# Layer B's transposition transfers issued by two queues, and its products with probabilities one sub-block later

## The chip, the cores and the metric

The kernel runs on one core of a Trainium2 chip. The core has five engines with instruction streams of their own: TensorE (PE in the profile, its weight loads PEld), VectorE (DVE), ScalarE (ACT), GpSimd (POOL) and SyncE (SP). Transfers run on 16 DMA engines; an engine's stream issues them, and the profile shows such issues with a q behind the engine's name (SPq, ACTq), those of GpSimd as POOL. The metric is the device time of one execution in microseconds (us), as the median of several runs.

## The reference

Two transformer layers over 256 positions of width 2048, with 32 heads of 128. Layer A has chunked attention with a relative bias. Layer B, the one that is changed, has "forgetting attention" against keys and values that come from a projection of their own:

```python
h_kv = rms_norm(x, kv_norm)
k_s, v_s = jnp.split(h_kv @ kv_w, 2, axis=-1)
logf = jax.nn.log_sigmoid((h_kv @ f_w + f_b).astype(jnp.float32))
cum_logf_h = jnp.transpose(jnp.cumsum(logf, axis=1), (0, 2, 1))
...
q, g = jnp.split(h @ b_w_in[lb], 2, axis=-1)
sc = einsum('bqhd,bkhd->bhqk', q_b, k_b) * scale + decay     # causal, decay from cum_logf_h
o = einsum('bhqk,bkhd->bqhd', softmax(sc), v_b)              # blocks of 128 queries
x = x + (o * silu(g)) @ b_w_out[lb]
```

All is in float32. The large products are made of three matmuls each, since every operand is split into a high part that TensorE takes whole and a low remainder: high by high, high by low, low by high.

## The kernel before

The kernel streams the weights once. Each layer's input projection is cut into 16 groups of two heads. A group has two **units** of 512 columns: in layer A `aqk` (queries and keys) and `avg` (values and gate), in layer B `bqg` (queries and gate) and `bkv` (keys and values). A unit has eight **sub-blocks** of 256 rows of the inner dimension, of 512 KB of weights each. From the second group on, seven of them are plain, and the eighth sub-blocks of the two units are done together as a **quad** (class `Quad`, lines 279 to 352): sums and differences of weight halves are formed, and fewer matmuls do both.

The way of a sub-block: SyncE issues its load (line 208) into one of six buffers `raw`; ScalarE makes the high part `hi` (line 244 in layer B, with the norm's gain; line 249 in A), VectorE the low part `lo` (line 245 or 250), each in one of four buffers, and TensorE multiplies (line 186). Splits are kept three sub-blocks ahead of TensorE. For the quad, ScalarE scales the raw weights (line 297), VectorE forms differences (lines 299, 300, 308, 309), and four splits follow (`quad_hi` line 305, `quad_lo` line 306).

Attention of a group runs as a side job, a Python generator that is advanced between the sub-blocks of later units. `side_b` (line 918) and `attention` (line 547) have these steps, each up to a `yield`:

1. `evac_scaled` copies the keys out, scaled (line 523), `turn` (line 509) transposes queries and keys: VectorE transposes 32 x 32 blocks into `first` (line 514), then sixteen transfers move the blocks into place in `sums` (line 517). The biases (lines 927, 928, 930) belong to this step.
2. `v_split` (lines 626 to 628): the values, split, into `vh`, `vl` and `v1`.
3. `split_pairs` (lines 535, 536): queries and keys split into `wide` and `q1`, and `q0` (line 559).
4. The scores: matmuls into `s1p` (lines 543 to 545) and `s0p` (line 567), then the first half of the softmax (lines 577 to 584), and its second half in a step of its own.
5. The gate is scaled by the softmax's sums (line 594), and a second `turn` transposes probabilities and gate together (from `sgY` to `sgZ`, again sixteen transfers).
6. `split` of the probabilities into `wide` (lines 535, 536).
7. The products with the probabilities into `op` (lines 543 to 545, 607).
8. The gate's multiplication and the split of the result (lines 611, 616, 617).

Where they run is set by hand. `drive` (line 744) advances a side by so many steps behind a sub-block. In layer B, `B1_STEPS = {3: 1, 5: 1, 6: 2}` puts step 2 behind sub-block 3 of the next group's first unit, step 3 behind sub-block 5, step 4 behind sub-block 6; `B2_STEPS = {1: 1}` puts step 5 into that group's second unit; `OLD_B_STEPS = {0: 1, 1: 99}` puts step 6 behind sub-block 0 of the first unit of the group after that, and steps 7 and 8 behind sub-block 1. The last two groups' sides run within the output projection (`project`, line 1022), with lists of counts.

The program's order in the code is not fully the order on the engines: an instruction may be moved ahead in its engine's stream where its data seem ready. Two devices bind it. `feed.behind` (line 264) writes a two-element copy of a weight split into a tile, so that what fills this tile comes behind that split; its place counts among the splits that are ready (0 to 2). `tc.issue_after(x)` puts what is traced within it behind `x` on the same engine, without an instruction. `feed.by_act` is ScalarE's last traced weight split.

Queues: in layer A, the first transposition's transfers go out by four queue entries (GpSimd three, ScalarE one), one for each `j`; in layer B all sixteen of both transpositions are issued by GpSimd. At a group's end, `add_whole` (line 731) adds the quad's part, held in `comb`, to the whole unit's result (VectorE, 128 x 512, line 735, twice), and `evac_scaled` then scales the keys (ScalarE, 128 x 256, line 523, twice).

Of the kernel before, what the change touches and what calls it, by code (L numbers as in the profile page):

```python
# [13 lines left out]
OP = mybir.AluOpType  # L14
# [4 lines left out]
NT = S // P  # L19
# [41 lines left out]
OLD_A_STEPS = {1: 1, 3: 99}  # L61
B1_STEPS = {3: 1, 5: 1, 6: 2}
B2_STEPS = {1: 1}
OLD_B_STEPS = {0: 1, 1: 99}
FORGET_STEPS = {0: 1, 2: 1, 6: 1, 7: 1}


def r32(ap):
    return ap.bitcast(F32)
# [8 lines left out]
def trunk(ctx, tc, x, x_t, gains, a_w_in, a_rel, a_w_out, kv_w, f_w, f_b, b_w_in, b_w_out, final_norm, out):  # L78
# [111 lines left out]
    class Feed:  # L190
# [73 lines left out]
        def behind(self, dst, n):  # L264

            act.activation(dst, r32(self.ready[n][0][:, 0, :, :1]), AF.Copy)

        def fill(self):
            while len(self.ready) <= DEPTH:
# [200 lines left out]
    def rest(u):  # L470

        for b in range(u.done, u.plain):
            u.step(b)
            yield u.acc
# [50 lines left out]
    def split_pairs(many, place=None):  # L525

        out = []
        for srcs, tag in many:
            out.append(att.tile([P, srcs[0].shape[1], 2, len(srcs), P], F32R, name=tag, tag=tag))
            if place is not None:  # L530
                feed.behind(out[-1][:, 0, 0, :, :1], place)
        for k in range(len(many[0][0])):
            for (srcs, _), both in zip(many, out):
                h, l = (both[:, :, i, k].rearrange("p t (i u) -> p t i u", u=SQ) for i in range(2))
                act.activation(h, srcs[k], AF.Copy)
                dve.tensor_sub(l, srcs[k], r32(h))  # L536
        return [[both[:, :, i].rearrange("p t k n -> p k n t") for i in range(2)] for both in out]

# [5 lines left out]
        pe.matmul(out_, a[0], b[1], start=False, stop=False)  # L544
        pe.matmul(out_, a[1], b[0], start=False, stop=stop)  # L545

    def attention(g, biases, qk, vg, half, ocat, queues=(pool,) * NQ, line=(None, None), home=None):


        z = turn(qk.rearrange("p t (c d) -> p (t c) d", d=DH), NT * 2 * HG, "qk", queues, home)  # L550
        bias1, bias0 = biases()
        qkT = z.rearrange("p i (t c) u -> p c t i u", t=NT)
        yield
        (kh, kl), (qh, ql) = split_pairs([([qkT[:, HG + i] for i in range(HG)], "wide"),
                                          ([qkT[:, i, 1:] for i in range(HG)], "q1")], line[0])
        q0 = att.tile([P, HG, P], F32, name="q0", tag="oT")
        if line[0] is not None:
            feed.behind(q0[:, :, :1], line[0])
        act.activation(q0.rearrange("p h (i u) -> p h i u", u=SQ),
                       qkT[:, :HG, 0], AF.Copy)  # L560
        yield
        s1p = bank("s1p")[:, :].rearrange("p (i s) -> p i s", i=HG)
        s0p = bank("s0p")[:, :HG * P].rearrange("p (i s) -> p i s", i=HG)
        for i in range(HG):
            dot3(s1p[:, i], (qh[:, i, :, 0], ql[:, i, :, 0]), (kh[:, i], kl[:, i]))
        for i in range(HG):
            pe.matmul(s0p[:, i], q0[:, i], qkT[:, HG + i, 0], start=True, stop=True)
        NB = 1 + NT
        sg = att.tile([P, HG * NB + NT * HG, P], F32, name="sg", tag="R")
        sv = sg[:, :HG * NB].rearrange("p (i c) k -> p i (c k)", i=HG)  # L570
        nm = small.tile([P, NT, HG], F32, name="nm")
        sm = small.tile([P, NT, HG], F32, name="sm")
        for t, sp_, s_, bias in ((1, s1p, sv[:, :, P:], bias1), (0, s0p, sv[:, :, :P], bias0)):
            if t:
                for i in range(HG):
                    to, plus = (v[:, i].rearrange("p (t n) -> p t n", t=NT) for v in (s_, bias))
                    dve.scalar_tensor_tensor(to, sp_[:, i].rearrange("p (n t) -> p t n", t=NT), SCALE, plus,
                                             op0=OP.mult, op1=OP.add)
            else:
                dve.scalar_tensor_tensor(s_, sp_, SCALE, bias, op0=OP.mult, op1=OP.add)  # L580
            dve.tensor_reduce(nm[:, t], s_, axis=AX.X, op=OP.max, negate=True)
            for i in range(HG):
                act.activation(s_[:, i], s_[:, i], AF.Exp, bias=nm[:, t, i:i + 1],  # L583
                               accum_out=sm[:, t, i:i + 1])
            if t:
                yield
        yield
        c = small.tile([P, NT, HG], F32, name="csc")
        dve.reciprocal(c, sm)
        dve.tensor_mul(c, c, half[:, :, None].to_broadcast([P, NT, HG]))  # L590
        (vh, vl, v1), gs = vg()
        for t in range(NT):
            for i in range(HG):
                act.activation(sg[:, HG * NB + t * HG + i], gs[:, t, i * DH:(i + 1) * DH], AF.Copy,
                               scale=c[:, t, i:i + 1])
        z = turn(sg, HG * NB + NT * HG, "sg")
        pT = z[:, :, :HG * NB].rearrange("p i (h c) u -> p h c i u", h=HG)
        gT = z[:, :, HG * NB:].rearrange("p i (t h) u -> p h t i u", t=NT)
        yield
        ph, pl = split([pT[:, i, :NT] for i in range(HG)], "wide", line[1])  # L600
        yield
        op = bank("op").rearrange("p (i s) -> p i s", i=HG)
        for i in range(HG):
            cols = slice(i * DH, (i + 1) * DH)
            dot3(op[:, i], (vh[:, cols], vl[:, cols]), (ph[:, i], pl[:, i]), i == 0, False)
        for i in range(HG):
            pe.matmul(op[:, i, 1::NT], v1[:, i * DH:(i + 1) * DH], pT[:, i, NT], start=False, stop=i == HG - 1)
        yield
        oT = att.tile([P, HG, S], F32, name="oT", tag="oT")
        for i in range(HG):  # L610
            dve.tensor_mul(oT[:, i].rearrange("p (t i u) -> p t i u", t=NT, u=SQ),
                           op[:, i].rearrange("p (i u t) -> p t i u", t=NT, u=SQ), gT[:, i])
        h0 = g * HG
        hi = ocat.hi[h0 // BIG][:, h0 % BIG:h0 % BIG + HG, :]
        lo = ocat.lo[h0 // BIG][:, h0 % BIG:h0 % BIG + HG, :]
        act.activation(hi, oT, AF.Copy)
        dve.tensor_sub(lo, oT, r32(hi))
        yield
# [299 lines left out]
    def side_b(g, accs):  # L918
        cb = att.tile([P, HG, S], F32, name="cb", tag="tb")
        sp.dma_start(out=cb, in_=bass.AP(tensor=cumd.tensor, offset=cumd.offset + g * HG * S,  # L920
                                           ap=[[0, P], [S, HG], [1, S]]))

        def biases():
            d0 = att.tile([P, HG, P], F32, name="d0")
            for i in range(HG):
                h = g * HG + i
                act.activation(d0[:, i], cb[:, i, :P], AF.Identity, bias=cum[:, 0, h:h + 1], scale=-1.0)
                act.activation(cb[:, i], cb[:, i], AF.Identity, bias=cum[:, 1, h:h + 1], scale=-1.0)
            for ap in (cb[:, :, P:], d0):
                pool.affine_select(out=ap, in_=ap, compare_op=OP.is_ge, fill=NEG, base=0,  # L930
                                   pattern=[[0, HG], [-1, P]], channel_multiplier=1)
            return cb, d0

        qk, gs = accs["q"]
        kv = accs["kv"]
        evac_scaled(kv, 0, GC, rsB, qk[:, :, GC:])
        rest_of = attention(g, biases, qk, lambda: (v, gs), halfB, oB, line=(1, 2), home=home)
        next(rest_of)
        yield
        v = v_split(kv, GC, rsB)  # L940
        yield
        yield from rest_of
# [8 lines left out]
    for g in range(NG):  # L951
        accs = {}
        if g:
            first, second = (Unit(x1T, next(order)) for _ in range(2))
            accs["qg"] = drive(rest(first), prev, B1_STEPS, {}, old, OLD_B_STEPS)

            def products():
                b_pairs[g - 1].step(x1T, first, second)
                open_b(accs, g)

            kv = drive(rest(second), prev, B2_STEPS, {QUAD_STEP_B - 1: products})
            accs["kv"] = add_whole(kv, 1)
        else:
            accs["qg"] = drive(unit(x1T), last[0], {2: 99})
            accs["kv"] = drive(unit(x1T), fg, FORGET_STEPS, {2: lambda: open_b(accs, g)})
            a_quads.sum_up(x1T, KD // KB - 1, sums[:, 0], a_quads.comb)
        old, prev = prev, side_b(g, accs)
        advance(prev)
# [42 lines left out]
    def bo_closed(u, acc):  # L1011
# [3 lines left out]
        for t in range(NT):  # L1015
# [3 lines left out]
            if u == 3:  # L1019
                finish_tile(t)  # L1020

    project(oB, bo, bo_order, bo_begun, bo_closed, [(old, [1, 1, 0]), (prev, [4, 2, 1, 1, 1, 7, 2, 1]),
                                                 (bo_quads.open(oB, QUADS), [20, 2, 2, 2, 2])])


# [43 lines left out]
```

## Time and profile before

| What | us |
|---|---|
| Median of three runs | 1781.92 (1781.47 to 1783.53) |
| The profiled execution, its own time | 1780.85 |
| Its span in the trace | 1779.1 |
| ScalarE, busy | 1197.0 |
| GpSimd, busy | 516.5 |

Layer A's groups run from the start to 695.3 us, its output projection to 860.3, layer B's groups to 1602.4, its output projection to the end. The mean granted clock of TensorE in the profiled execution was 0.998. A row of a group of instructions reads: line, engine, operation, written tile <- read tiles, shape, count, busy time, mean duration in ns, then the idle time of the engine ahead of them and what ended it. In the view of waits a row reads: who waited <- for whom: total us, times, longest us. In the view in order of time a row reads: start, length, engine, line, operation, tiles, shape, count, and in brackets the idle time ahead of it with what ended it. Rows of TensorE overlap: a matmul of 512 columns is shown as 0.38 us long, while its successor may start 0.22 us behind its start.

### The profile page before, as it was taken

The numbers are of one execution on the slowest core, as the hardware profiler recorded it, in microseconds if no ns is written. First come the engines' busy times: TensorE is split into PE (matmuls) and PEld (weight loads), VectorE is DVE, ScalarE is ACT, GpSimd is POOL, SyncE is SP. The second block draws the span as 40 slices with busy tenths as digits, with TensorE's granted clock in tenths as the row PEclk, the third lists the DMA queues.
The fourth block names the chain that finished last, engine by engine and source line by source line (L and its number), as shares of the span: only waits on it lengthen the run. The fifth ranks groups of instructions, "written<-read, shape, count | busy, mean of one in ns | idle before, by whom it ended". The sixth has DMA issues, their size and how long they took to land.

```text
span 1779.1 us, 26149 instructions
## 1 busy us (share of the span) xinstructions
PE 1738.7 (98%) x8258; PEld 1508.9 (85%) x8258; DVE 1493.1 (84%) x2252; ACT 1197.0 (67%) x2227; POOL 516.5 (29%) x1071
## 2 busy tenths in 40 slices
PE   9999999999999999999999999999999999999997
PEld 7888888888888888888887888888887888888886
DVE  7888888888888888888868888888888888886887
ACT  6666666666666666556667777777777777775554
POOL 2333333333333333111123333333333333333000
PEclk9999999999999999999999999999999999999999
DMA  8776777677776667676756666666666666667754
GB/s 311 243 227 223 231 227 228 221 227 230 228 228 223 222 224 241 223 260 223 252 193 208 214 216 222 221 217 212 215 211 203 213 215 209 224 208 238 236 199 144
DMA packets 143146, 396.38 MB, mean 223 GB/s; under 512 B 31104, under 2 KB 37536, under 8 KB 142880
## 3 DMA queue, kind: packets, MB, share of 16 engines
q1 hardware_dynamic: 106960, 354.25, 60.8%
q0 software_dynamic: 32256, 37.29, 6.5%
q10 hardware_dynamic: 3792, 3.17, 0.6%
q8 instruction: 65, 1.06, 0.2%
q14 instruction: 73, 0.60, 0.1%
HBM read 351.05 MB, written 4.23 MB: 200 GB/s over the span
## 4 chain that ended last, share of the span: by engine, by line
PE 72%; DVE 12%; ACT 10%; issue 4%; DMA 2%; POOL 0%; DVEq 0%; SPq 0%; ACTq 0%
PE avg_acc L186 16%; PE aqk_acc L186 16%; PE bqg_acc L186 11%; PE bo_acc L186 7%; PE ao_acc L186 7%; PE bkv_acc L186 4%; DVE bqg_lo L245 3%; DVE bkv_lo L245 3%; ACT bkv_hi L244 2%; ACT quad_hi L305 2%; DVE comb L735 2%; PE p L544 1%; PE p L543 1%; PE p L545 1%; ACT sg L583 1%
## 5 line engine op out<-in xcount | busy, mean ns | idle before, releaser
L517 POOL DMA_DIRECT2D sums<-first x448 | 220.0, 498 | 355.5 <-DVE wide L536 219.0
L517 POOL DMA_DIRECT2D sgZ<-sgY x512 | 251.0, 497 | 190.8 <-DVE sgY L514 95.7
L245 DVE SCALAR_TENSOR_TENSOR bkv_lo<-bkv_raw,gain,bkv_hi 128x512 fp32r<-128x512 f32 x226 | 158.4, 748 | 21.9 <-ACT bkv_hi L244 20.2
L186 PE MATMUL aqk_acc<-aqk_hi,xTh 128*128 128x512 f32 x452 | 168.1, 384 | 0.2 <-ACT aqk_hi L249 0.2
L186 PE MATMUL bkv_acc<-bkv_hi,x1Th 128*128 128x512 f32 x452 | 168.1, 383 | 0.0
L186 PE MATMUL avg_acc<-avg_hi,xTh 128*128 128x512 f32 x452 | 167.4, 382 | 0.0
L186 PE MATMUL bqg_acc<-bqg_hi,x1Th 128*128 128x512 f32 x452 | 167.4, 382 | 0.0
L186 PE MATMUL aqk_acc<-aqk_lo,xTh 128*128 128x512 f32 x452 | 166.3, 379 | 0.9 <-DVE aqk_lo L250 0.9
L249 ACT ACTIVATE avg_hi<-avg_raw 128x1024 fp32r<-128x1024 f32 x112 | 116.2, 1051 | 75.6 <-PE avg_acc L186 50.0
L244 ACT ACTIVATE bqg_hi<-bqg_raw,gain 128x512 fp32r<-128x512 f32 x226 | 149.2, 712 | 26.4 <-PE bqg_acc L186 8.8
L186 PE MATMUL bkv_acc<-bkv_hi,x1Tl 128*128 128x512 f32 x452 | 166.6, 380 | 0.0
L186 PE MATMUL bkv_acc<-bkv_lo,x1Th 128*128 128x512 f32 x452 | 166.5, 380 | 0.0
L186 PE MATMUL aqk_acc<-aqk_hi,xTl 128*128 128x512 f32 x452 | 166.1, 379 | 0.0
L186 PE MATMUL bqg_acc<-bqg_lo,x1Th 128*128 128x512 f32 x452 | 166.1, 379 | 0.0
L186 PE MATMUL avg_acc<-avg_lo,xTh 128*128 128x512 f32 x452 | 166.1, 379 | 0.0
L186 PE MATMUL avg_acc<-avg_hi,xTl 128*128 128x512 f32 x452 | 166.1, 379 | 0.0
L186 PE MATMUL bqg_acc<-bqg_hi,x1Tl 128*128 128x512 f32 x452 | 166.1, 379 | 0.0
L245 DVE SCALAR_TENSOR_TENSOR bqg_lo<-bqg_raw,gain,bqg_hi 128x512 fp32r<-128x512 f32 x226 | 158.7, 748 | 8.6 <-ACT bqg_hi L244 8.6
L250 DVE TENSOR_TENSOR avg_lo<-avg_raw,avg_hi 128x1024 fp32r<-128x1024 f32 x112 | 136.7, 1221 | 31.1 <-ACT avg_hi L249 31.1
L244 ACT ACTIVATE bkv_hi<-bkv_raw,gain 128x512 fp32r<-128x512 f32 x226 | 144.8, 710 | 19.8 <-PE bqg_acc L186 17.5
L250 DVE TENSOR_TENSOR aqk_lo<-aqk_raw,aqk_hi 128x1024 fp32r<-128x1024 f32 x110 | 134.2, 1223 | 25.4 <-ACT aqk_hi L249 20.4
L249 ACT ACTIVATE aqk_hi<-aqk_raw 128x1024 fp32r<-128x1024 f32 x110 | 115.6, 1051 | 42.2 <-PE avg_acc L186 26.8
(382 smaller groups left out, 4350.5 us busy)
## 6 DMA issues: line engine op xcount, KB each, us to landing
bqg_raw<-in_b_w_in SPq DMA_DIRECT2D x128, 512.0 KB, 4.7
bkv_raw<-in_kv_w SPq DMA_DIRECT2D x128, 512.0 KB, 4.4
avg_raw<-in_a_w_in SPq DMA_DIRECT2D x127, 512.0 KB, 4.6
aqk_raw<-in_a_w_in SPq DMA_DIRECT2D x125, 512.0 KB, 4.5
ao_raw<-in_a_w_out SPq DMA_DIRECT2D x64, 512.0 KB, 4.8
bo_raw<-in_b_w_out SPq DMA_DIRECT2D x64, 512.0 KB, 4.4
sgZ<-sgY POOLq DMA_DIRECT2D x512, 40.0 KB, 4.5
sums<-first POOLq DMA_DIRECT2D x448, 32.0 KB, 3.8
```

Of the source, the lines that this page charges most:

```text
L186: pe.matmul(acc[t], x[:, t * P:(t + 1) * P], w, start=t not in begun, stop=last and i == 2)
L244: self.by_act = act.activation(hi[:, j], raw[:, j], AF.Copy, scale=gk)
L245: self.by_dve = dve.scalar_tensor_tensor(lo[:, j], raw[:, j], gk, r32(hi[:, j]), op0=OP.mult, op1=OP.subtract)
L249: self.by_act = act.activation(hi[:, j], raw[:, j], AF.Copy)
L250: self.by_dve = dve.tensor_sub(lo[:, j], raw[:, j], r32(hi[:, j]))
L305: feed.by_act = act.activation(hi[:, :n], src, AF.Copy)
L517: queues[j].dma_start(out=r32(z)[j * SQ:(j + 1) * SQ, i], in_=y[i * SQ:(i + 1) * SQ, j])
L543: pe.matmul(out_, a[0], b[0], start=start, stop=False)
L544: pe.matmul(out_, a[0], b[1], start=False, stop=False)
L545: pe.matmul(out_, a[1], b[0], start=False, stop=stop)
L583: act.activation(s_[:, i], s_[:, i], AF.Exp, bias=nm[:, t, i:i + 1], accum_out=sm[:, t, i:i + 1])
L735: dve.tensor_add(out[t], acc[t], out[t])
```

## The change

Layer B's `attention` now gets queues for both transpositions, `(pool, sp) * 2`: for each block row `i`, the transfers with even `j` are issued by GpSimd and those with odd `j` by SyncE, eight and eight. The products with probabilities (step 7, with step 8) run behind sub-block 2 and not 1, and likewise in the output projection. The places of the splits in steps 3 and 6, ready split 1 and 2 before, become "last": behind ScalarE's last traced weight split, by `issue_after` and without the two-element copies. From the second group on, the keys' part of `comb` is scaled ahead, in the hook behind the quad (ScalarE, two 128 x 256), so that at the group's end VectorE writes the keys in one step each (two 128 x 256 `scalar_tensor_tensor`) and adds the values' half apart (two 128 x 256 additions), and ScalarE's copies there are gone. Layer A keeps its queues, places and steps.

```diff
-OLD_B_STEPS = {0: 1, 1: 99}
+OLD_B_STEPS = {0: 1, 2: 99}
...
+        def after(self, place):
+
+            return tc.issue_after(self.by_act.ins) if place == "last" else nullcontext()
...
-            if place is not None:
+            if place is not None and place != "last":
                 feed.behind(out[-1][:, 0, 0, :, :1], place)
...
-                act.activation(h, srcs[k], AF.Copy)
+                with feed.after(place):
+                    act.activation(h, srcs[k], AF.Copy)
...
-    def attention(g, biases, qk, vg, half, ocat, queues=(pool,) * NQ, line=(None, None), home=None):
+    def attention(g, biases, qk, vg, half, ocat, queues, line, home, turned=(pool,) * NQ):
...
-        if line[0] is not None:
+        if line[0] != "last":
             feed.behind(q0[:, :, :1], line[0])
-        act.activation(q0.rearrange("p h (i u) -> p h i u", u=SQ),
-                       qkT[:, :HG, 0], AF.Copy)
+        with feed.after(line[0]):
+            act.activation(q0.rearrange("p h (i u) -> p h i u", u=SQ), qkT[:, :HG, 0], AF.Copy)
...
-        z = turn(sg, HG * NB + NT * HG, "sg")
+        z = turn(sg, HG * NB + NT * HG, "sg", turned)
...
-        evac_scaled(kv, 0, GC, rsB, qk[:, :, GC:])
-        rest_of = attention(g, biases, qk, lambda: (v, gs), halfB, oB, line=(1, 2), home=home)
+        if g:
+            for t in range(NT):
+                whole_ = a_quads.comb[:, NT + t]
+                dve.scalar_tensor_tensor(qk[:, t, GC:], kv[t][:, :GC], rsB[:, t:t + 1], whole_[:, :GC],
+                                         op0=OP.mult, op1=OP.add)
+            for t in range(NT):
+                whole_ = a_quads.comb[:, NT + t]
+                dve.tensor_add(whole_[:, GC:], kv[t][:, GC:], whole_[:, GC:])
+            kv = [a_quads.comb[:, NT + t] for t in range(NT)]
+        else:
+            evac_scaled(kv, 0, GC, rsB, qk[:, :, GC:])
+        rest_of = attention(g, biases, qk, lambda: (v, gs), halfB, oB, (pool, sp) * (NQ // 2), ("last", "last"), home, (pool, sp) * (NQ // 2))
...
                 open_b(accs, g)
-
-            kv = drive(rest(second), prev, B2_STEPS, {QUAD_STEP_B - 1: products})
-            accs["kv"] = add_whole(kv, 1)
+                for t in range(NT):
+                    k = a_quads.comb[:, NT + t, :GC]
+                    act.activation(k, k, AF.Copy, scale=rsB[:, t:t + 1])
+
+            accs["kv"] = drive(rest(second), prev, B2_STEPS, {QUAD_STEP_B - 1: products})
...
-    project(oB, bo, bo_order, bo_begun, bo_closed, [(old, [1, 1, 0]), (prev, [4, 2, 1, 1, 1, 7, 2, 1]),
+    project(oB, bo, bo_order, bo_begun, bo_closed, [(old, [1, 2, 0]), (prev, [4, 2, 1, 1, 1, 7, 2, 1]),
```

## The prediction

> **What bounds the kernel now.** I read the page first, then the same amount of work in layer A and in layer B side by side, then who waits for whom in layer B, then the instructions in order of time around each wait of TensorE. The page:
>
> ```profile
> span 1779.1 us, 26149 instructions
> ...
> PE 1738.7 (98%) x8258; PEld 1508.9 (85%) x8258; DVE 1493.1 (84%) x2252; ACT 1197.0 (67%) x2227; POOL 516.5 (29%) x1071
> ```
>
> TensorE is the bound, and 98% seems to leave nothing. The next view gives eight head groups of layer A (265.0 to 609.2) and eight of layer B (1045.8 to 1415.6): length of the stretch, busy time and count of matmuls, then the other engines.
>
> ```profile
> 265.00:609.20 344.20, 344.20 (x1673) 303.67 (x1673) 295.95 (x410) 223.60 (x401) 111.13 (x232) 1.00 0.71 229
> 1045.80:1415.60 369.80, 355.49 (x1673) 304.45 (x1672) 313.50 (x522) 280.69 (x584) 132.88 (x272) 1.00 0.66 214
> ```
>
> The same 1673 matmuls at the same granted clock of 1.00 take 344.2 us in A and 369.8 us in B. B loses 25.6/8 = 3.2 us per group, 15 × 3.2 = 48 us over the fifteen groups whose waits the view after it gives (907 to 1602 us). Only 14.3 us of the 25.6 count as idle; the rest hides in the busy time, as a matmul that starts late also restarts the pipeline. So a stall is to be measured from start to start. The waits of layer B (who waited for whom, total us, times, longest):
>
> ```profile
> ACT wide L535 <- DMA sums<-first: 61.7, 15, 5.6
> ...
> ACT qk L523 <- DVE comb L735: 39.5, 29, 2.0
> ...
> PE bqg_acc L544 <- DVE quad_lo L306: 10.2, 14, 0.8
> ...
> PE op L544 <- DVE wide L536: 7.7, 13, 0.7
> ...
> PE s1p L543 <- ACT q L535: 3.4, 5, 0.9
> ...
> PEld s0p L567 <- issue: 3.2, 14, 0.2
> PE s1p L545 <- DVE q L536: 3.1, 9, 0.4
> ACT v L628 <- PE op L607: 3.0, 13, 0.3
> ```
>
> TensorE waits at three places: the products with probabilities (op), the scores (s1p, s0p) and the quad step (bqg_acc L544). The first row is the odd one: in each of the fifteen groups ScalarE stands 4.1 us at the head of its stream for the transfers of the first transposition, and everything queued behind it stands too.
>
> **The op step, moved.** TensorE in order of time, one group of A, then one of B (start, us, instruction):
>
> ```profile
> 385.23 0.27 PE L543 MATMUL op<-wide,vh 128*128 128x256 f32 x1
> ...
> 386.26 0.46 PE L186 MATMUL avg_acc<-avg_hi,xTh 128*128 128x512 f32 x1
> ...
> 1234.98 0.27 PE L543 MATMUL op<-wide,vh 128*128 128x256 f32 x1
> ...
> 1237.13 0.46 PE L186 MATMUL bqg_acc<-bqg_hi,x1Th 128*128 128x512 f32 x1
> ```
>
> The ten matmuls take 1.03 us in A and 2.15 us in B: 1.12 us lost, in the fourteen groups that the loop runs it in, 15.7 us. The missing piece is the low half of the probabilities, under 1 us late. The new step count puts op one sub-block of twelve matmuls later, 12 × 0.22 = 2.6 us (spacing from the next fence), more than twice the loss. I take all 15.7 us. What moves along: the copies of V into vh and v (L626, L628) may overwrite only after op, and wait 0.23 us for it now (3.0/13). They can wait up to 2.6 us longer on ScalarE; the 3.46 us that ScalarE idles a little later (below) cover that, and without this cover it would come back in the scores. The output's own multiplications move along; nothing reads them before the output projection.
>
> **The scores.** The quad step's loss first:
>
> ```profile
> 1262.73 0.38 PE L545 MATMUL bkv_acc<-quad_hi,sums 128*128 128x512 f32 x1
> 1262.95 0.38 PE L543 MATMUL bqg_acc<-quad_hi,x1Th 128*128 128x512 f32 x1
> 1264.07 0.48 PE L544 MATMUL bqg_acc<-quad_lo,x1Th 128*128 128x512 f32 x1 [0.74 <-DVE quad_lo L306]
> ```
>
> 1.12 us between starts where 0.22 is usual, so 0.9 lost, and 0.1 more by which the delayed matmul itself runs longer (0.48 against 0.38): 1.0 us, 15 groups, 15 us. So the scores hold the remainder, 48 - 15.7 - 15 = 17.3 us. Their cause, in one group:
>
> ```profile
> 1234.33 1.24 DVE L514 STREAM_TRANSPOSE first<-qk 128x1024 f32<-128x1024 f32 x1
> ...
> 1236.11 5.39 POOL L517 DMA_DIRECT2D sums<-first  x11 [6.75 <-PE bqg_acc L186]
> ...
> 1244.57 0.50 POOL L517 DMA_DIRECT2D sums<-first  x1 [0.91 <-DMA sums<-first]
> ...
> 1243.84 0.19 ACT L266 ACTIVATE wide<-bkv_hi 128x2 fp32r<-128x2 f32 x1
> ...
> 1247.68 0.42 ACT L535 ACTIVATE wide<-sums 128x256 fp32r<-128x256 f32 x1 [3.46 <-DMA sums<-first]
> ...
> 1248.51 1.32 ACT L244 ACTIVATE bkv_hi<-bkv_raw,gain 128x512 fp32r<-128x512 f32 x2
> ```
>
> VectorE is done at 1235.57, GpSimd needs until 1245.07 for sixteen issues (0.49 us each, plus waits for earlier ones to land), and ScalarE goes on only at 1247.68. For the new split, the price of a small issue on another queue and the landing times:
>
> ```profile
> 380.89 2.44 ACTq L517 DMA_DIRECT2D sums<-first  x4
> ```
>
> ```profile
> L208 SPq DMA_DIRECT2D bqg_raw<-in_b_w_in x113: 327/328/332, 912.3 to 1563.6; - x113
> ```
>
> ```profile
> bqg_raw<-in_b_w_in SPq DMA_DIRECT2D x128, 512.0 KB, 4.7
> ...
> sums<-first POOLq DMA_DIRECT2D x448, 32.0 KB, 3.8
> ```
>
> SyncE does none of these now. Its eight cost between 8 × 0.33 = 2.6 us (its own weight loads) and 8 × 0.61 = 4.9 us (the same transfer issued by ScalarE in A); I take 4.9, being the same shape. GpSimd's eight cost 3.9. Both start about 0.5 us after the transposition, so the last issue is at 1241.0 and lands 3.8 to 4.7 us later, at 1244.8 to 1245.7: 2 to 3 us earlier than now. Also the ScalarE part ahead of the transposition goes:
>
> ```profile
> L735 DVE TENSOR_TENSOR comb<-bkv_acc,comb x28: 676/682/693, 954.5 to 1558.5; 128x512 f32<-128x512 f32 x28
> ```
>
> ```profile
> L523 ACT ACTIVATE qk<-comb,rstd_b x58: 489/507/512, 948.0 to 1599.8; 128x256 f32<-128x256 f32 x58
> ```
>
> ```profile
> L639 DVE SCALAR_TENSOR_TENSOR gs<-gs,comb x30: 409/419/605, 949.9 to 1601.1; 128x256 f32<-128x256 f32 x30
> ```
>
> Two additions of 0.68 and two copies of 0.51 become four half-wide VectorE steps, for which 0.42 of the nearest row stands: VectorE does 0.3 us more per group, and the chain to the transposition loses up to 1.0 us. ScalarE does the scaling of K earlier, 2 × 0.51 in the products hook, where it waits for VectorE anyway (39.5 us over 29 waits). If that cover were gone it would cost 1 us per group of ScalarE, not of TensorE. I count none of this.
>
> The place "last" drops four marker copies (0.19 us each) per group; the scores' splits now stand behind one more weight split of 1.32 us. In the order of work this is the split at 1248.51, which today runs in between. From 1244.8 to 1245.7 the data wait for ScalarE and not the reverse. The stall of the scores is that lateness; I take 90% of 17.3 = 15.5 us and keep 0 and 17.3 as ends. The reading engines wait on more semaphores, since the data come over two queues; s0p pays 3.2/14 = 0.23 us for such issue time now, doubled at worst 3.4 us in all, and nothing when TensorE no longer arrives at a stalled instruction.
>
> **The quad step.** What ends its wait:
>
> ```profile
> 1260.48 0.49 ACT L928 ACTIVATE cb<-cb,cum 128x256 f32<-128x256 f32 x1
> ...
> 1261.71 1.04 ACT L305 ACTIVATE quad_hi<-bqg_raw 128x1024 fp32r<-128x1024 f32 x1
> ...
> 1262.79 1.23 DVE L306 TENSOR_TENSOR quad_lo<-bqg_raw,quad_hi 128x1024 fp32r<-128x1024 f32 x1 [0.43 <-ACT quad_hi L305]
> ```
>
> ScalarE is late here because it has been catching up since 1247.68; but three bias steps stand ahead of the last quad split, and the second transposition and its transfers come here too. ScalarE's data come 2 to 3 us earlier while TensorE gains 17.3/15 = 1.2 us in the scores, so ScalarE gets 0.8 to 1.8 us ahead of it and the 1.0 us could go. As the order of the bias steps may come out anew, I take half, 7.5 us, with 0 and 15 as ends.
>
> **Sum.** 15.7 + 15.5 + 7.5 = 38.7 us. The profiled execution took 1780.85 us (span 1779.1); 1780.85 - 38.7 = 1742.2. The median of the runs lies 1.07 above that execution, so 1743. With all 48 us gone it is 1734.
>
> **SyncE's queue.** The eight issues add a wait for VectorE's transposition to the queue of the weight loads; behind them stand the loads, for which ScalarE's splits wait. Behind the second transposition, whose transfers GpSimd begins at 1262.34, it is tightest:
>
> ```profile
> 1262.39 10.27 SPq L208 DMA_DIRECT2D bqg_raw<-in_b_w_in  x6
> ```
>
> ```profile
> 1268.04 1.34 ACT L244 ACTIVATE bqg_hi<-bqg_raw,gain 128x512 fp32r<-128x512 f32 x2
> ```
>
> ```profile
> 1275.61 0.38 PE L186 MATMUL bqg_acc<-bqg_hi,x1Th 128*128 128x512 f32 x1
> ```
>
> ```profile
> 1262.34 3.93 POOL L517 DMA_DIRECT2D sgZ<-sgY  x8 [0.54 <-issue]
> 1266.67 2.44 POOL L517 DMA_DIRECT2D sgZ<-sgY  x5 [0.40 <-DMA sgZ<-sgY]
> ```
>
> SyncE is issuing for 6 × 0.33 = 2 of these 10.3 us. The first load lands at about 1262.39 + 4.7 = 1267.1; with the high split's 1.34 us, and as much again for the low one (an estimate), it is ready at 1269.8, and TensorE reads it at 1275.61. A delay of 5.8 us costs TensorE nothing; 4.9 us lies inside.
>
> **Rivals.** (1) *The split over two queues buys nothing*; only the moved step pays. For it: the landing of 4.7 us on SyncE's queue against 3.8, and the splits' later place. The Trainium skill says (DMA: Bandwidth & Descriptors, "Issuing engines are not separate DMA queues") that starting transfers from several engines saves only the sequencer's time to start them, usually small beside the transfer. By that rule the time would be this rival's. The trace disagrees on "small": sixteen issues take 9.0 us here, a landing 3.8. The time: 1781.9 - 15.7 = 1766. Chance 0.14.
>
> (2) *The relief moves into the quad step*: TensorE gets there earlier and ScalarE, tied up by the biases, does not, so the loss of 1.0 us grows by half: 1781.9 - 15.7 - 15.5 + 7.5 = 1758. For it: the wait is about the same in fourteen groups, 0.73 us in the mean and 0.8 at most. Against: the catching up goes. Chance 0.12.
>
> (3) *Slower: weight loads stuck on SyncE.* GpSimd's ninth transfer waits for an earlier one to land (the row x8, then x5 with its wait). If SyncE's issues and the loads share such a limit, the loads come 4.9 + 4.7 = 9.6 us late: TensorE stands 9.6 - 5.8 = 3.8 us per group, 57 us, and the result is 1781.9 - 38.7 + 57 = 1800. It comes out slower than before from a delay of 5.8 + 38.7/15 = 8.4 us. Against: SyncE is idle four fifths of that stretch. Chance 0.09.
>
> (4) *The order does not come out as written*: the bias steps of the next group run ahead of the quad split, so the streams are not in the code's order, and op or the splits may end up as late as before: 1782. Chance 0.05.
>
> **Numbers.** My forecast (1734 to 1752) has 0.60. The range 1733 to 1767 holds it and rivals 1 and 2, except their upper tails, and leaves out 3 and 4. Faster by over 0.2% (about what a measurement of this kernel can tell): 0.86; within 0.2%: 0.05; slower: 0.09.
>
> **What would show it.** Right: the eight-group stretch of B falls from 369.8 to about 349 us with 1673 matmuls; op to the next L186 takes about 1.03 us; the wait of wide L535 for DMA sums<-first, 61.7 us now, is under 15; the last sums<-first issue ends about 5 us, not 9.5, after the transposition. The quad wait tells between forecast and rival 2. Wrong: bqg_hi or bkv_hi on ScalarE waiting for raw weights, TensorE waiting at L186 for the splits (rival 3), or the DMA wait of L535 as long as now (rival 1).

## The result and the profile after

| Kernel | median us | lowest to highest |
|---|---|---|
| before | 1782.65 | 1781.47 to 1783.53 |
| after | 1732.09 | 1731.21 to 1732.73 |

The ratio is 0.9716, with a 95% interval of 0.9700 to 0.9733: 50.6 us less. The profiled execution of after took 1731.21 us. It comes out faster, as forecast, but by 11.9 us more than the 38.7 of the sum, and 0.9 us below the range. The page of after:

```profile
span 1729.5 us, 26618 instructions
PE 1714.6 (99%) x8258; PEld 1505.1 (87%) x8258; DVE 1499.0 (87%) x2282; ACT 1186.5 (69%) x2163; POOL 394.7 (23%) x815
```

The same 8258 matmuls. The eight-group stretch of layer B and then the fifteen groups, of after (columns as before):

```profile
908.00:1552.80 644.80, 644.63 (x3127) 568.27 (x3126) 589.32 (x993) 515.93 (x1034) 136.09 (x272) 1.00 0.66 230
1036.00:1380.70 344.70, 344.53 (x1673) 303.65 (x1672) 317.06 (x537) 275.32 (x553) 72.14 (x144) 1.00 0.66 229
```

and the fifteen groups of before:

```profile
907.40:1602.40 695.00, 667.83 (x3128) 571.22 (x3126) 584.12 (x965) 524.91 (x1091) 250.25 (x512) 1.00 0.66 213
```

1673 matmuls of layer B now take 344.7 us, against 369.8 before and 344.2 in layer A. The fifteen groups went from 695.0 to 644.8 us: these 50.2 us are the whole gain, since the span of the profiled executions fell by 49.6 (1779.1 to 1729.5). Every wait that TensorE has left in the whole program of after (who waited for whom, total us, times, longest):

```profile
PE heat L112 <- DVE zeros L109: 1.3, 1, 1.3
PE bo_acc L549 <- DVE quad_lo L310: 1.2, 1, 1.2
PE aqk_acc L186 <- ACT aqk_hi L249: 1.0, 1, 1.0
PE ao_acc L549 <- DVE quad_lo L310: 1.0, 2, 0.7
PE aqk_acc L186 <- DVE aqk_lo L250: 0.7, 1, 0.7
PE ao_acc L548 <- ACT quad_hi L309: 0.3, 1, 0.3
PE ao_acc L186 <- ACT ao_hi L249: 0.2, 1, 0.2
PE bo_acc L186 <- DVE bo_lo L250: 0.2, 1, 0.2
PE op L612 <- DMA sums<-first: 0.2, 1, 0.2
```

Only the last row lies in layer B's groups; quad step, scores and op no longer wait. Around a first transposition of after, in order of time:

```profile
1211.90 1.24 DVE L518 STREAM_TRANSPOSE first<-qk 128x1024 f32<-128x1024 f32 x1
...
1213.22 5.34 SPq L521 DMA_DIRECT2D sums<-first  x8
...
1213.68 3.92 POOL L521 DMA_DIRECT2D sums<-first  x8 [14.47 <-issue]
...
1222.84 1.33 ACT L244 ACTIVATE bkv_hi<-bkv_raw,gain 128x512 fp32r<-128x512 f32 x2 [1.25 <-issue]
1224.08 0.40 ACT L540 ACTIVATE wide<-sums 128x256 fp32r<-128x256 f32 x1
```

The last issue ends 5.4 us after the transposition (9.5 before), and ScalarE's first split (L540) follows its weight split with no wait for a transfer, where before it stood 3.46 us. The row of these waits, 61.7 us before, is gone from the view. op, in after:

```profile
1216.29 0.27 PE L548 MATMUL op<-wide,vh 128*128 128x256 f32 x1
...
1217.33 0.46 PE L186 MATMUL bqg_acc<-bqg_hi,x1Th 128*128 128x512 f32 x1
```

1.04 us from its start to the next weight matmul, as in layer A (1.03).

### The profile page after: what moved, and what is told of

The parts are those of the page before. It is cut to its first block, busy times and chain, and to the rows that moved or that the text cites. A ratio compares the mean times of both kernels' runs of the same rounds, so it can differ in the third digit from the quotient of the medians.

```text
span 1729.5 us, 26618 instructions
## 1 busy us (share of the span) xinstructions
PE 1714.6 (99%) x8258; PEld 1505.1 (87%) x8258; DVE 1499.0 (87%) x2282; ACT 1186.5 (69%) x2163; POOL 394.7 (23%) x815
## 4 chain that ended last, share of the span: by engine, by line
PE 96%; DVE 1%; DMA 1%; ACT 1%; issue 0%; SPq 0%; POOL 0%; ACTq 0%; DVEq 0%
PE bkv_acc L186 17%; PE avg_acc L186 17%; PE bqg_acc L186 17%; PE aqk_acc L186 16%; PE bo_acc L186 8%; PE ao_acc L186 7%; PE p L549 2%; PE p L548 2%; PE p L550 2%; PE op L612 1%; PE s0p L572 1%; DMA bo_raw<-in_b_w_out 0%; PE s1p L550 0%; PE s1p L549 0%; PE s1p L548 0%; PE op L550 0%
## 5 line engine op out<-in xcount | busy, mean ns | idle before, releaser
L521 POOL DMA_DIRECT2D sums<-first x320 | 157.3, 499 | 432.8 <-issue 157.8
L521 POOL DMA_DIRECT2D sgZ<-sgY x384 | 188.1, 497 | 154.5 <-DVE sgY L518 96.0
L245 DVE SCALAR_TENSOR_TENSOR bkv_lo<-bkv_raw,gain,bkv_hi 128x512 fp32r<-128x512 f32 x226 | 162.0, 764 | 18.2 <-ACT bkv_hi L244 17.8
L186 PE MATMUL aqk_acc<-aqk_hi,xTh 128*128 128x512 f32 x452 | 167.5, 382 | 1.0 <-ACT aqk_hi L249 1.0
L186 PE MATMUL bkv_acc<-bkv_hi,x1Th 128*128 128x512 f32 x452 | 167.5, 382 | 0.0
L186 PE MATMUL bqg_acc<-bqg_hi,x1Th 128*128 128x512 f32 x452 | 167.4, 382 | 0.0
L186 PE MATMUL avg_acc<-avg_hi,xTh 128*128 128x512 f32 x452 | 167.4, 382 | 0.0
L186 PE MATMUL aqk_acc<-aqk_lo,xTh 128*128 128x512 f32 x452 | 166.3, 379 | 0.7 <-DVE aqk_lo L250 0.7
L186 PE MATMUL bqg_acc<-bqg_hi,x1Tl 128*128 128x512 f32 x452 | 166.1, 379 | 0.0
L186 PE MATMUL avg_acc<-avg_hi,xTl 128*128 128x512 f32 x452 | 166.1, 379 | 0.0
L186 PE MATMUL bqg_acc<-bqg_lo,x1Th 128*128 128x512 f32 x452 | 166.1, 379 | 0.0
L186 PE MATMUL bkv_acc<-bkv_hi,x1Tl 128*128 128x512 f32 x452 | 166.1, 379 | 0.0
L186 PE MATMUL bkv_acc<-bkv_lo,x1Th 128*128 128x512 f32 x452 | 166.1, 379 | 0.0
L186 PE MATMUL aqk_acc<-aqk_hi,xTl 128*128 128x512 f32 x452 | 166.1, 379 | 0.0
L186 PE MATMUL avg_acc<-avg_lo,xTh 128*128 128x512 f32 x452 | 166.1, 379 | 0.0
```

The costliest lines, as they stand in the source:

```text
L186: pe.matmul(acc[t], x[:, t * P:(t + 1) * P], w, start=t not in begun, stop=last and i == 2)
L245: self.by_dve = dve.scalar_tensor_tensor(lo[:, j], raw[:, j], gk, r32(hi[:, j]), op0=OP.mult, op1=OP.subtract)
L521: queues[j].dma_start(out=r32(z)[j * SQ:(j + 1) * SQ, i], in_=y[i * SQ:(i + 1) * SQ, j])
```

## The experiments

All were timed against the kernel before in three rounds (its median beside the first four was 1780.0 us, beside the next four 1781.6, beside the last four 1781.4); ratios have 95% intervals. Three theories:

- **L (landing).** The last landing of the *first* transposition paces ScalarE. Let it come early, and scores and quad step both stop waiting; places and keys matter little.
- **P (places and keys).** The new places of the splits and the keys scaled ahead free ScalarE, and give a large part.
- **H (held loads).** The transfers land sooner mainly because SyncE's weight loads are held back, not because a second queue issues half of them.

| Experiment | median us | ratio to before |
|---|---|---|
| a_queues: before, both transpositions over two queues | 1749.14 | 0.9822 (0.9804 to 0.9841) |
| a_step: before, op one sub-block on | 1787.95 | 1.0045 (1.0029 to 1.0062) |
| u_queues: after, all on GpSimd | 1752.47 | 0.9845 (0.9826 to 0.9864) |
| u_step: after, op back at sub-block 1 | 1769.20 | 0.9934 (0.9915 to 0.9953) |
| h_hold: after, all on GpSimd, SyncE held | 1785.58 | 1.0023 (1.0014 to 1.0033) |
| f_first: after, only the first transposition split | 1731.14 | 0.9718 (0.9703 to 0.9732) |
| f_second: after, only the second split | 1777.00 | 0.9978 (0.9968 to 0.9987) |
| s_all: after, all on SyncE | 1795.72 | 1.0081 (1.0058 to 1.0103) |
| q1_step: before, first split and op one on | 1731.89 | 0.9729 (0.9708 to 0.9750) |
| p_place: u_queues without the keys | 1772.00 | 0.9949 (0.9935 to 0.9962) |
| p_keys: u_queues without the places | 1773.35 | 0.9962 (0.9948 to 0.9975) |
| v_both: f_first, layer A's transposition split too | 1738.92 | 0.9765 (0.9745 to 0.9786) |

**The queues alone** (a_queues; `attention` also gets the `turned` argument):

```diff
-        rest_of = attention(g, biases, qk, lambda: (v, gs), halfB, oB, line=(1, 2), home=home)
+        rest_of = attention(g, biases, qk, lambda: (v, gs), halfB, oB, (pool, sp) * (NQ // 2), (1, 2), home, (pool, sp) * (NQ // 2))
```

> The kernel before with the queues of both transpositions alone. Theory L (the landing of the first transposition's transfers holds ScalarE, and ScalarE's lateness makes both the scores' and the quad step's stalls): the wait of wide L535 for these transfers falls from 61.7 us to under 10, scores and quad stalls go, op's 15 us remain, 1748 to 1752 us. Theory P (the places in ScalarE's stream and the keys' copies make the stalls): little changes, 1775 to 1782 us.

1749.1 us, about 31 less than its before and inside L's range. All that TensorE still waits for in its layer B:

```profile
PE op L544 <- DVE wide L536: 4.3, 10, 0.9
PE op L607 <- issue: 3.6, 10, 0.4
PE op L607 <- DMA bkv_raw<-in_kv_w: 1.8, 5, 0.4
```

The waits of scores *and* quad step are gone, with places, keys and op as before. So the split of the transfers ends both, and the gain is about the whole of both: 17.3 + 15 = 32.3 by the prediction's losses. Which of the two transpositions makes it is tried below.

**The step alone** (a_step):

```diff
-OLD_B_STEPS = {0: 1, 1: 99}
+OLD_B_STEPS = {0: 1, 2: 99}
...
-    project(oB, bo, bo_order, bo_begun, bo_closed, [(old, [1, 1, 0]), (prev, [4, 2, 1, 1, 1, 7, 2, 1]),
+    project(oB, bo, bo_order, bo_begun, bo_closed, [(old, [1, 2, 0]), (prev, [4, 2, 1, 1, 1, 7, 2, 1]),
```

> The kernel before with op one sub-block later alone. As the prediction's sum has it, the terms add up: 15.7 us less, 1766 us. Theory L says the scores stay tied to the landing, so TensorE only arrives there 1.1 us earlier per group and waits that much longer: op's stall goes, the scores' grows, 1776 to 1782 us.

1788.0: slower, and above both expectations. Its waits:

```profile
ACT wide L535 <- DMA sums<-first: 78.5, 15, 7.8
...
PE s1p L543 <- ACT q L535: 14.0, 16, 2.4
PE bqg_acc L544 <- DVE quad_lo L306: 8.1, 11, 0.8
```

No row of op is left, yet ScalarE waits for the landing for 78.5 us where it was 61.7, (78.5 - 61.7)/15 = 1.12 us more per group: just what op set free, given back at the scores, whose first row grew from 3.4 to 14.0 us. That explains no gain. Why it is worse than none stays open; the last transfer lands 13.0 us after the transposition here, 12.7 in before (medians over the groups), which may be a part of it.

**All on GpSimd** (u_queues):

```diff
-        rest_of = attention(g, biases, qk, lambda: (v, gs), halfB, oB, (pool, sp) * (NQ // 2), ("last", "last"), home, (pool, sp) * (NQ // 2))
+        rest_of = attention(g, biases, qk, lambda: (v, gs), halfB, oB, (pool,) * NQ, ("last", "last"), home)
```

> The changed kernel with all sixteen transfers of both transpositions on GpSimd again. Theory L: ScalarE stands for the landing again, scores and quad stalls are back, 1755 to 1780 us. Theory P: 1732 to 1740 us.

1752.5: without the split, some 20 us of after's gain are gone and 28 stay. That is 2.5 us below L's range and far from P's. ScalarE's wait is back, smaller, with the quad's and a part of the scores':

```profile
PE bqg_acc L549 <- DVE quad_lo L310: 8.5, 14, 0.7
PE s1p L548 <- ACT q L540: 2.5, 4, 1.5
```

```profile
ACT wide L540 <- DMA sums<-first: 35.9, 16, 4.6
```

**op back at sub-block 1** (u_step): the a_step diff reversed on after.

> The changed kernel with op back behind sub-block 1 (and in the output projection). As the prediction has it, op's 1.12 us per group come back and nothing else does: 1747 to 1749 us. Rival: the keys' copies that left ScalarE had made the probabilities late, so op does not wait even there: 1732 to 1736 us.

1769.2, outside both expectations: the step is worth 37 us here, not 15.7:

```profile
PE op L549 <- DVE wide L541: 18.2, 14, 2.3
PE op L612 <- DMA sums<-first: 5.8, 15, 0.5
```

op waits 18.2/14 = 1.3 us, against 4.3/10 = 0.4 in a_queues, from which u_step differs in places and keys alone: with op early these two *cost* 20 us. "Last" puts the probabilities' split behind one more weight split; whether it is that or the keys was not separated.

**Which transposition** (f_first, f_second): in the diff of u_queues the second line has, for f_first, `(pool, sp) * (NQ // 2)` first and nothing last; for f_second `(pool,) * NQ` first and `(pool, sp) * (NQ // 2)` last.

> The changed kernel with the first transposition alone on two queues, the second all on GpSimd again. Theory L (the landing of the first transposition makes both stalls): neither the scores' nor the quad step's stall comes back, 1731 to 1738 us. Theory Q (the quad step's stall comes from the second transposition's transfers): 1.0 us per group comes back, 1745 to 1750 us.

> The changed kernel with the second transposition alone on two queues, the first all on GpSimd again. Theory L: as with all on GpSimd, 1748 to 1756 us. Theory Q: the quad step's stall stays away, 1733 to 1740 us.

f_first is at 1731.1, as fast as after: beside the first split, the second gives nothing. f_second is at 1777.0, 24.5 us above u_queues and outside both expectations: without the first split, the second is a loss. Its waits on ScalarE:

```profile
ACT wide L540 <- DMA sums<-first: 52.9, 15, 5.5
ACT bqg_hi L244 <- DMA bqg_raw<-in_b_w_in: 20.8, 8, 3.5
```

The weights come late behind the second transposition's issues (u_queues and f_first have no such row), and the wait for the first one's landing is 17 us longer than in u_queues. Read from the two traces as medians over the groups, the first transposition ends 5.5 us behind the last matmul of keys and values, not 4.4, and its last transfer lands 13.7 us after it, not 13.0. That is 1.8 us per group, 27 over fifteen, about the loss; why the transposition itself comes later is not shown. So L holds for what the first landing does, by f_first, but it left out what the held loads cost.

**Held loads** (h_hold): u_queues' queues, and beside both transpositions SyncE issues eight transfers of 32 x 128 bytes into a tile that nothing reads, so that its loads are held without its helping.

```diff
+    held = const.tile([P, NQ, SQ], F32, name="held")
...
+                if hold and j % 2:
+                    sp.dma_start(out=held[j * SQ:(j + 1) * SQ, i], in_=y[i * SQ:(i + 1) * SQ, j, 0])
```

> The changed kernel with all sixteen transfers of each transposition on GpSimd, and eight small transfers of the same transposed tile (32 partitions x 128 bytes, into a tile that nobody reads) issued by SyncE between them, so that SyncE's weight loads stand for as long as in the changed kernel. Theory H (the transfers land sooner because the weight loads are held back meanwhile): the median landing falls from 4.4 us, as it was with all sixteen on GpSimd, to 2 to 2.6 us, and the time from 1752 to 1735 to 1745 us. Theory I (only the halved issue time counts): the landing stays at 4 us or more, and the time at 1750 us or above.

1785.6, 33 us slower than u_queues. The transfers `sums<-first` from issue to landing, first in u_queues, then here (the 4.4 of the expectation counts those of the second transposition too):

```profile
DMA to landing us min/median/max: 1.7/4.1/6.8
```

```profile
DMA to landing us min/median/max: 1.6/2.5/6.5
```

H has the median right and the time wrong: the loads, once released, come as a burst beside the later transfers. In order of time:

```profile
1096.70 6.09 SPq L526 DMA_DIRECT2D held<-first  x8
1102.90 0.52 SPq L208 DMA_DIRECT2D bkv_raw<-in_kv_w  x1
1103.52 0.38 SPq L208 DMA_DIRECT2D bqg_raw<-in_b_w_in  x1
1103.99 3.70 SPq L208 DMA_DIRECT2D bkv_raw<-in_kv_w  x4
```

```profile
1097.22 3.45 POOL L523 DMA_DIRECT2D sums<-first  x7 [11.34 <-issue]
1102.19 4.41 POOL L523 DMA_DIRECT2D sums<-first  x9 [1.52 <-issue]
```

Seven go out while SyncE is held, nine mostly beside the burst. ScalarE waits for the last one, not for the median, and that one lands 13.6 us after the transposition (13.0 in u_queues), so the held queue buys no time. It costs some: the loads stand behind the second transposition as well, and as in f_second the first one ends later, 5.7 us behind the last matmul of keys and values. That fewer issues on each engine bring the last landing forward, and not faster transfers, is seen in a_queues (3.3 us in the median, the last landing at 7.2) and in the next run.

**All sixteen on SyncE** (s_all): `(sp,) * NQ` for both.

> The changed kernel with all sixteen transfers of both transpositions on SyncE. By the issue time of 0.59 us, sixteen take 9.5 us or more and the last lands 11 to 12 us after the transposition, as late as before: theory L then has the scores' and quad stalls back, 1750 to 1775 us. Rival 3 of the prediction (weight loads stuck on SyncE make TensorE stand) would show here first: the loads come 9 to 10 us late, beyond the slack of 5.8 us, TensorE waits for splits at L186, 1780 us or above.

1795.7, the side on which the prediction's third rival would have come out. A transfer lands as fast as in after (1.9 us in the median), yet the sixteen issues end 10.2 us after the transposition, and the last landing comes at 11.5 (medians over the groups). The issues also hold the weight loads:

```profile
ACT bqg_hi L244 <- DMA bqg_raw<-in_b_w_in: 45.1, 20, 4.6
ACT wide L540 <- DMA sums<-first: 28.0, 14, 2.9
```

```profile
PE bqg_acc L548 <- ACT quad_hi L309: 11.8, 12, 1.5
PE bqg_acc L549 <- DVE quad_lo L310: 10.8, 14, 0.8
PE op L549 <- DVE wide L541: 7.7, 9, 1.3
```

TensorE's waits for splits at L186, by which the third rival would have lost its time, are 2.2 us in all fifteen groups; the time goes at the quad step and at op. Eight issues stay hidden, sixteen do not.

**Two edits only** (q1_step): the kernel before with the diff of a_step, and that of a_queues without its last argument.

> The kernel before with two edits alone: the first transposition's transfers on two queues, and op one sub-block later; the places, the keys and the second transposition as before. If these two make the whole gain: 1731 to 1736 us. If the places or the keys are needed as well: 1740 us or above.

1731.9, all of after's gain. TensorE's only wait in its layer B:

```profile
PE bqg_acc L544 <- DVE quad_lo L306: 0.8, 1, 0.8
```

Places, keys and the second split add nothing to this.

**Places or keys without the split** (p_place, p_keys): u_queues with the keys' part as in before, and with the places `(1, 2)`.

> All transfers on GpSimd; op one sub-block later and the places "last", the keys as before. The step alone took 1788 us, step, places and keys together 1752 us. If the places make these 36 us (a weight split of ScalarE no longer stands behind the wait for the transfers): 1752 to 1762 us. If the keys do: 1780 us or above.

> All transfers on GpSimd; op one sub-block later and the keys' scaling ahead, the places 1 and 2 as before. If the keys make the 36 us (the transposition, and with it the landing, comes up to 1 us earlier): 1752 to 1762 us. If the places do: 1775 to 1788 us.

1772.0 and 1773.4, where a_step (neither) is at 1788.0 and u_queues (both) at 1752.5: 15 to 16 us each, some 35 together. Neither edit makes the 36 us alone, so both results lie between the ranges given. For the keys the trace shows how: the transposition ends 4.4 us behind the last matmul of keys and values in p_keys and u_queues, 5.45 in a_step and p_place (medians over the groups), and 15 × 1.0 us is about what the edit gives. So P is true while the landing is late. Once it is early, places and keys add nothing with op late (q1_step against after), and cost 20 us with op early (u_step).

**The same for layer A** (v_both): f_first, and layer A's queues `(pool, sp) * (NQ // 2)` for `(pool, pool, pool, act)`.

> The changed kernel with the second transposition back on GpSimd, and layer A's first transposition also half on GpSimd and half on SyncE (its last quarter was on ScalarE's queue). Layer A's TensorE waits sum to a few us only, so at most 4 us can come of it: 1727 to 1732 us. If the held weight loads cost layer A, whose ScalarE waits for raw weights already before: 1733 to 1745 us.

1738.9, 7.8 us above f_first, as the second range has it. Layer A's groups end at 703.8 us, in f_first at 695.2, so the whole loss lies there. In layer A (0 to 700 us), of before and then of v_both:

```profile
DVE first L300 <- DMA avg_raw<-in_a_w_in: 8.9, 14, 2.2
```

```profile
DVE first L304 <- DMA avg_raw<-in_a_w_in: 31.5, 14, 3.8
```

Layer A's TensorE waited for no landing before, so there was nothing to gain, and behind the eight issues the weights for its quad's differences come later. No kernel tried is clearly faster than after; f_first and q1_step equal it with less changed.

## Why the prediction was right, and where it was wrong

**The step that failed** is the quad's term, "As the order of the bias steps may come out anew, I take half, 7.5 us, with 0 and 15 as ends." All 15 went. The quad step in after:

```profile
1235.60 0.50 ACT L933 ACTIVATE cb<-cb,cum 128x256 f32<-128x256 f32 x1
...
1236.86 1.06 ACT L309 ACTIVATE quad_hi<-bqg_raw 128x1024 fp32r<-128x1024 f32 x1
...
1237.94 1.23 DVE L310 TENSOR_TENSOR quad_lo<-bqg_raw,quad_hi 128x1024 fp32r<-128x1024 f32 x1 [0.43 <-ACT quad_hi L309]
```

```profile
1240.11 0.38 PE L549 MATMUL bqg_acc<-quad_lo,x1Th 128*128 128x512 f32 x1
```

The order of the bias steps did not come out anew: they stand ahead of the last quad split as before. The low part is ready at 1237.94 + 1.23 = 1239.17 and is read at 1240.11, 0.9 us later, and so it is in most of the fifteen groups; before, TensorE lost 0.9 us there. So ScalarE's lead grew by some 1.8 us, the top of the 0.8 to 1.8 us that the prediction had itself worked out, and more than the 1.0 us lost there. So the term was 15 us and not 7.5. a_queues shows such a lead (0.6 to 0.9 us in all fifteen groups), and no wait at the quad, with places, keys and op as in before.

**The other misses.** 90% of the scores' loss was taken and all of it went (1.8 us), and fifteen groups lost 50.2 us, not 15 × 3.2 = 48: a sample of eight groups was scaled up (2.2 us). With the quad's 7.5 this is 11.5 of the 11.9 us by which the gain went beyond the sum.

**The terms do not stand alone.** With the landing early the step is worth 17.3 us (a_queues 1749.1 to q1_step 1731.9) for the 15.7 forecast. Alone it costs 8 (1788.0 against 1780.0 of before beside it): the prediction priced three stalls as independent, while those of scores and quad step are one lateness of ScalarE, into which a gain at op runs. That op's term came near is owed to the split made with it, a condition that the prediction did not name. In the same way it counted the keys at nothing and was right, though they are worth 15 us while the landing is late.

**The landing** was shorter than forecast. The transfers of after:

```profile
L521 SPq DMA_DIRECT2D sums<-first x120: 507/588/1856, 910.2 to 1519.8; - x120
...
DMA to landing us min/median/max: 1.7/1.9/4.9
```

An issue on SyncE costs 0.59 us, 8 × 0.59 = 4.7, near the 4.9 taken. The landing takes 1.9 us in the median, not 3.8 to 4.7, and the last one comes 7.0 us after the transposition (median over the groups, each transfer's issue and landing taken from the trace), where 9.2 to 10.1 was forecast and 12.7 was before. By the same working it is 6.6 to 7.2 us in the six kernels that split the first transposition (after, a_queues, u_step, f_first, q1_step, v_both), and 12.7 to 13.7 in the seven that leave it to GpSimd (before, a_step, u_queues, f_second, h_hold, p_place, p_keys).

**Rivals.** The first (nothing from the split) is out. The Trainium skill's rule behind it (DMA: Bandwidth & Descriptors, "Issuing engines are not separate DMA queues") names the right saving, the sequencer's time to start a transfer, and calls it usually small beside the transfer. For one transfer the trace agrees (0.50 us on GpSimd against a landing of 3.8); the prediction set sixteen issues against one landing. But sixteen in a row are not small: the end of the issues moved from 9.5 to 5.4 us. The second (quad grows) is out, and so is the fourth (order of the streams): op, scores and quad step all come without a wait. The third's sign came, without its price:

```profile
ACT bqg_hi L244 <- DMA bqg_raw<-in_b_w_in: 27.4, 12, 3.5
```

ScalarE waits up to 3.5 us for weights, and in these groups TensorE never for ScalarE: the slack of 5.8 us held. These waits come from the second transposition's issues alone, for f_first and q1_step, which leave those on GpSimd, have no such row. s_all and v_both show where borrowing SyncE's queue begins to cost.

## What to carry to other kernels

Where an in-order engine stands at the head of its queue for transfers, find the *last* landing of that batch and ask who issues it and how long the issuing takes; here a second issuer for one batch and one moved step made the whole gain. Do not add up stalls that have one late engine behind them: test the early one first, since a step that frees time only ahead of the other wait gives it back there. And borrow a load queue only as far as the buffered work lasts: eight issues were free in layer B, sixteen were not, and eight were not in layer A.

## What the runs showed of the hardware

- The landing time of the same 32 KB transfer differed from kernel to kernel: 4.1 us in the median with all sixteen on GpSimd and SyncE's weight loads running beside them (u_queues), 1.9 with SyncE issuing half of them (after), 2.5 with SyncE merely held (h_hold). It is not the held loads alone: a_queues, with the same split as after, has a median of 3.3 and nearly the same last landing (7.2 us, after 7.0). What sets it was not tried.
- SyncE needs 0.59 us to issue a 32 KB transfer between tiles (after) and 0.33 for a 512 KB weight load (before); GpSimd needs 0.50 for the first (before).
- Idle time of TensorE counted too little here: eight groups of before lost 25.6 us against layer A, of which 14.3 show as idle.
